# TensorE's order in two mixers: from the scheduler's to the emitted one, with new constants in the estimate behind it

## The chip, the cores and the metric

The kernel runs on one core of a Trainium2 chip. The metric is the device time of one execution in microseconds. Before the change the median of three runs is 2134.4 us (2134.18 to 2135.02). One further execution was profiled; every row shown comes from it.

The engines have short names in the rows: PE is TensorE's matrix products, PEld its weight loads, DVE is VectorE, ACT ScalarE, POOL GpSimd and SP the engine that issues the DMAs.

## The reference

The reference is a trunk of two layers for a sequence of 512 tokens of width 1024, in float32. A layer adds to its state half a gated feed-forward, then a mixer, then half a second gated feed-forward:

```
for layer in range(2):
    x = x + 0.5 * swiglu_ffn(x, pre weights)        # 1024 -> 2 x 2816 -> 1024
    u = rms_norm(x, mix_norm)
    x = x + mixer(u) @ w_out                        # A in layer 0, B in layer 1
    x = x + 0.5 * swiglu_ffn(x, post weights)
    if layer == 0: k_blocks, v_blocks = shared_kv_blocks(x)
```

Mixer A projects `u`, shifts the result by a token, and runs a linear recurrence over the 512 tokens for 12 heads of width 64:

```
sa    = einsum(state, -kk_t)
state = state * w_t + sa * (kk_t * a_t) + v_t * k_t
y_t   = einsum(state, r_t)
```

The output is normed per head and gated. Four more heads attend over 256 memory tokens. Mixer B has 12 heads of windowed attention with three dilations on the shared keys and values, and four memory heads.

## The kernel before

**Layout.** The state stands transposed, 128 features on the partitions and 512 tokens along them, in eight tiles. Every large product is split: a float32 operand becomes a high and a low part, and three products (high by high, high by low, low by high) are summed in PSUM. `dense` emits these triples. For each chunk of four 128 x 128 weight blocks it calls `weight`, which loads the raw chunk (SP, six buffers), copies it to `whi` on ScalarE and subtracts to `wlo`, on GpSimd in the mixers (four buffers each). After each triple it yields once.

**Mixer A.** The 12 heads are six pairs, called heads here. The recurrence is done in chunks of 64 tokens. `rwkv_prepare` makes the scaled operands of a head, `rwkv_solve` inverts a triangular matrix in five doubling levels, `rwkv_finish` steps through the eight chunks and norms the result. One level of the solve is: a transposition on VectorE (`tx<-TT`), sixteen 64 x 64 products on TensorE (`sc<-tx,mb`), a masked copy on VectorE (`tx<-sc,cst`), sixteen more products (`sc<-TT,tx`), and an addition on VectorE (`TT<-TT,sc`). Each float32 product stands in the trace as two rows, hence 32 rows to a block.

The mixer's work is written as eight generators, or strands: finish, two scans (solves of even and odd heads), prepare, two of memory attention, the projections, and a first pass of the output projection. `prepare` for head j waits until head j-2 is finished (`len(ys) > j - 2`), and the projections of head j wait until head j-2 is prepared.

**Mixer B.** Here the strands are memory attention, two of dilated attention, `settle` (norms and transpositions of the projections), the projections, and a first pass of the output projection.

**The order.** `weave` picks the strand to emit from. A strand that yields `WAIT` names the time at which its last results are expected; one that yields `FREE` can go on at once. The first strand in the list whose time has come is taken, and if there is none, the one that comes next. Time here is an estimate: `Meter` holds a clock for each of the four computing engines, and for each tile when it was last written and read. `note` advances them at each emitted instruction: it starts when its engine is free and its inputs are written, in the order of emission on every engine, and takes what `cost` says. The clock of TensorE is the present time of `weave`. DMAs and the loading of ScalarE's function tables are not in the estimate.

```
start = max([self.clock[engine], self.read.get(name, 0.0)] + [self.written.get(a.tensor.name, 0.0) for a in ins])
end = start + self.cost(engine, op, out, ins, sum(a.shape[-1] == 1 for a in ins))
```

**The compile-time scheduler.** The emitted program then goes through the scheduler of the language. It replays the program with a cost model of its own and gives each engine, whenever it is free there, the first emitted instruction that is ready. So an instruction can be moved ahead of earlier emitted ones. What comes out is a fixed order for each engine; on the chip an instruction waits for its semaphores, and those behind it on that engine wait with it. Before the change this holds for TensorE too. The feed-forward stages are emitted straight, without `weave`.

All instructions of the computing engines stand in the trace under line 278, that of the recording helper `Engine`; rows are told apart by their tiles: `mm` are the projections' PSUM tiles, `sc` those of the small steps, `py` those of the recurrence and of the attention outputs, `fps` those of the feed-forward; `uh`, `ul` and `kvh`, `kvl` are the split activations.

## Time and profile before

| | |
|---|---|
| median of three runs | 2134.4 us |
| the profiled execution: its time, its span | 2133.36 us, 2131.6 us |
| TensorE busy (products; weight loads) | 2065.4 us; 1651.9 us |
| VectorE, ScalarE, GpSimd busy | 983.3, 817.6, 583.1 us |
| mean granted clock of TensorE | 0.995 |
| instructions | 32197 |

The span runs from the first to the last instruction of the trace; the execution's own time has a little around it. Mixer A lies at about 385 to 800 us, mixer B at about 1545 to 1785 us, and the rest is feed-forward and the memory and key work beside it. A row that groups instructions gives their count, then busy time in us and the mean of one in ns, then the idle time just before them and what ended it. A row in order of time gives the start and the duration in us. Products overlap in TensorE's pipeline, so the distance of two starts says more than a duration.

### The profile page before, as it was taken

The page shows a single profiled execution, that of the slowest core. Times are in us where ns is not written, and L with a number is a line of the kernel's source. Part 1 is how long each engine was busy: PE and PEld are TensorE (multiplying, and loading weights), DVE is VectorE, ACT ScalarE, POOL GpSimd, SP SyncE. Part 2 cuts the span into 40 slices and gives each one's busy share as a digit, 9 for nine tenths or more (in the row PEclk, how much of TensorE's full clock was granted, in tenths as well). Part 3 has the DMA queues.
Part 4 walks back from the last instruction along what each step waited for, and adds up shares of the span by engine and source line. Part 5 has one row for each costly group of instructions (what it writes and reads, how often), then busy time and mean ns, then how long its engine had stood idle before and what let it go on. Part 6 is the DMA issues. An engine that isn't in the chain of part 4 may idle for free.

```text
span 2131.6 us, 32197 instructions
## 1 busy us (share of the span) xinstructions
PE 2065.4 (97%) x12734; PEld 1651.9 (77%) x12734; DVE 983.3 (46%) x1354; ACT 817.6 (38%) x1408; POOL 583.1 (27%) x502
## 2 busy tenths in 40 slices
PE   8999999979989899999999999999999999999999
PEld 6888888857666577778888888888877667888887
DVE  6333343575767747333434533324376675333322
ACT  6333333423333545333433433333345654333321
POOL 2222222643332133222222222222242224222221
PEclk9999999999999999999999999999999999999999
DMA  5322344311100045253344423234441144222342
GB/s 194 97 97 96 92 136 126 117 46 34 34 27 24 24 152 188 93 183 99 109 127 126 158 95 98 95 94 135 125 136 50 38 161 156 96 97 96 94 136 82
DMA packets 130632, 221.90 MB, mean 104 GB/s; under 512 B 14232, under 2 KB 31824, under 8 KB 130480
## 3 DMA queue, kind: packets, MB, share of 16 engines
q1 hardware_dynamic: 130480, 219.83, 32.8%
q8 instruction: 100, 1.64, 0.3%
q14 instruction: 52, 0.43, 0.1%
HBM read 202.89 MB, written 21.61 MB: 105 GB/s over the span
## 4 chain that ended last, share of the span: by engine, by line
PE 62%; DVE 2%; ACT 1%; issue 1%; DMA 0%; POOL 0%; SPq 0%; POOLq 0%; ACTq 0%; DVEq 0%
PE fps L278 50%; PE mm L278 6%; PE sc L278 4%; PE py L278 1%; DMA xin<-xd 0%; DVE prob L278 0%; DVE x L278 0%; DVE tmp L278 0%; DVE ul L278 0%; ACT krv L278 0%; DVE wlo L278 0%; DVE dmx L278 0%; POOL wlo L278 0%; DVE mpr L278 0%; ACT tmp L278 0%
## 5 line engine op out<-in xcount | busy, mean ns | idle before, releaser
L278 POOL TENSOR_TENSOR wlo<-raw,whi 128x512 fp32r<-128x512 f32 (+3 forms) x404 | 496.3, 1230 | 1439.7 <-ACT whi L278 1395.2
L278 ACT ACTIVATE whi<-raw 128x512 fp32r<-128x512 f32 (+3 forms) x684 | 416.1, 610 | 955.1 <-PE fps L278 778.7
L278 PE MATMUL fps<-uh,whi 128*128 128x512 f32 x1408 | 551.9, 392 | 7.6 <-ACT whi L278 7.6
L278 PE MATMUL fps<-uh,wlo 128*128 128x512 f32 x1408 | 550.0, 391 | 4.0 <-DVE wlo L278 2.4
L278 PE MATMUL fps<-ul,whi 128*128 128x512 f32 x1408 | 549.2, 390 | 0.0
L278 DVE TENSOR_TENSOR wlo<-raw,whi 128x512 fp32r<-128x512 f32 x280 | 201.2, 719 | 347.0 <-ACT whi L278 337.3
L278 PEld LDWEIGHTS fps<-uh,whi 128*128 128x128 f32 x1408 | 264.9, 188 | 68.3 <-ACT whi L278 11.1
L278 PEld LDWEIGHTS fps<-uh,wlo 128*128 128x128 f32 x1408 | 264.9, 188 | 62.0 <-DVE wlo L278 4.1
L278 PEld LDWEIGHTS fps<-ul,whi 128*128 128x128 f32 x1408 | 265.0, 188 | 56.0 <-issue 0.7
L278 PE MATMUL fps<-hh,whi 128*128 128x512 f32 x704 | 273.9, 389 | 0.0
L278 PE MATMUL fps<-hl,whi 128*128 128x512 f32 x704 | 273.9, 389 | 0.0
L278 PE MATMUL fps<-hh,wlo 128*128 128x512 f32 x704 | 273.9, 389 | 0.0
L278 DVE TENSOR_TENSOR gs<-fps,rstd 128x512 f32<-128x512 f32 x88 | 60.5, 690 | 322.9 <-PE fps L278 322.9
L278 PEld LDWEIGHTS fps<-hh,whi 128*128 128x128 f32 x704 | 132.1, 188 | 27.5
L278 PEld LDWEIGHTS fps<-hh,wlo 128*128 128x128 f32 x704 | 132.1, 188 | 27.4
L278 PEld LDWEIGHTS fps<-hl,whi 128*128 128x128 f32 x704 | 132.1, 188 | 27.4
L278 PE MATMUL mm<-uh,whi 128*128 128x512 f32 x280 | 120.6, 431 | 1.3 <-DVE x L278 0.9
L278 DVE TENSOR_TENSOR hm<-fps,gs 128x512 f32<-128x512 f32 x88 | 60.6, 691 | 121.5 <-PE fps L278 115.8
L278 PE MATMUL mm<-ul,whi 128*128 128x512 f32 x280 | 114.7, 410 | 1.1 <-DVE ul L278 1.1
L278 PE MATMUL mm<-uh,wlo 128*128 128x512 f32 x280 | 113.3, 405 | 0.0
L278 DVE RECIPROCAL tmp<-tmp 128x128 f32<-128x128 f32 x112 | 97.8, 918 | 29.1 <-ACT tmp L278 29.0
L278 DVE TENSOR_TENSOR hl<-hm,hh 128x512 fp32r<-128x512 f32 x88 | 76.9, 877 | 50.7 <-ACT hh L278 50.7
(256 smaller groups left out, 2115.5 us busy)
## 6 DMA issues: line engine op xcount, KB each, us to landing
raw<-w SPq DMA_DIRECT2D x512, 256.0 KB, 2.7
raw<-wa_in SPq DMA_DIRECT2D x44, 256.0 KB, 3.0
xd<-x SPq DMA_DIRECT2D x40, 256.0 KB, 3.8
tmp<-xd SPq DMA_DIRECT2D x32, 256.0 KB, 3.7
xin<-xd SPq DMA_DIRECT2D x32, 256.0 KB, 4.2
raw<-w_kv SPq DMA_DIRECT2D x24, 256.0 KB, 2.8
raw<-w SPq DMA_DIRECT2D x32, 128.0 KB, 2.3
raw<-wmem SPq DMA_DIRECT2D x16, 256.0 KB, 2.6
```

Of the source, the lines that this page charges most:

```text
L278: r = f(*args, **kw)
```

## The change

Two things change together.

- In `mixer_a` and `mixer_b` a manual schedule is opened for TensorE: inside it the scheduler keeps TensorE's instructions in the order in which they are emitted. The other engines are ordered by the scheduler as before, and so is TensorE outside the two mixers.
- The constants of `Meter.cost` are new, and so is the time from the end of an instruction to the use of its result: 0.22 us for all engines, where it was 0.2 for VectorE and 0.15 for the others. With the constants, the emitted order of both mixers changes, since `weave` goes by them.

```
             if op == "transpose":
-                return n * 0.00083 + 0.003
+                return n * 0.00083 + 0.013
             passes = 4 if ins[1].dtype == F32 else 1
             small = self.ways > 1
-            turn, self.small = 0.1 * (small != self.small), small
-            return turn + max(n * passes * 0.000417, 0.105) / self.ways + 0.003
+            turn, self.small = 0.09 * (small != self.small), small
+            return turn + (max(n * passes * 0.000417, 0.096) + 0.013) / self.ways
         if engine == "scalar":
-            return (0.05 if psum else 0.09) + 0.08 * extra + n * 0.00083
+            return (0.16 if psum else 0.21) + 0.08 * extra + n * 0.0008
         if engine == "gpsimd":
-            return 0.1 + n * (0.0022 if op.startswith("tensor_tensor") else 0.001)
+            return 0.19 + n * (0.00215 if op.startswith("tensor_tensor") else 0.001)
         if op == "reciprocal":
-            return 0.07 + n * 0.0063
-        fast = op in ("tensor_scalar", "tensor_copy") and not psum
-        return 0.07 + 0.06 * extra + n * (0.00052 if fast else 0.00104)
+            return 0.07 + n * 0.0064
+        if op in ("tensor_scalar", "tensor_copy") and not psum:
+            return 0.27 + n * 0.0003
+        return 0.142 + 0.06 * extra + n * (0.0021 if op == "tensor_tensor_scan" else 0.00107)
...
-        late = end + (0.15 if engine != "vector" else 0.2)
+        late = end + 0.22
...
     def mixer_a(...):
             pool = ctx.enter_context(tc.tile_pool(name="mixa", bufs=1, reuse_waits="tile"))
+            ctx.enter_context(tc.manual_schedule(engines={mybir.EngineType.PE}))
...
     def mixer_b(...):
             pool = ctx.enter_context(tc.tile_pool(name="mixb", bufs=1, reuse_waits="tile"))
+            ctx.enter_context(tc.manual_schedule(engines={mybir.EngineType.PE}))
```

## The prediction, on record before the result

> **What bounds the kernel now.** I read the totals first, then the forty slices, the busy time by stretches, the groups of instructions, and last the order of time inside one solve of mixer A.

> ```profile
> span 2131.6 us, 32197 instructions
> PE 2065.4 (97%) x12734; PEld 1651.9 (77%) x12734; DVE 983.3 (46%) x1354; ACT 817.6 (38%) x1408; POOL 583.1 (27%) x502
> PE   8999999979989899999999999999999999999999
> ```

> TensorE sets the time; the low digits stand in slices 9 to 15, which is mixer A. By stretches (us; then busy time and count of PE, weight loads, VectorE, ScalarE, GpSimd; granted clock; DMA):

> ```profile
> 420.00:720.00 300.00, 266.45 (x4035) 195.10 (x4033) 201.48 (x282) 100.95 (x179) 107.17 (x98) 0.97 0.10 31
> 720.00:750.00 30.00, 25.43 (x351) 17.74 (x352) 23.00 (x52) 19.93 (x51) 0.00 (x0) 1.00 0.12 37
> 1545.00:1755.00 210.00, 199.31 (x1075) 147.80 (x1075) 144.54 (x212) 110.40 (x210) 58.75 (x50) 1.00 0.30 93
> 675.00:700.00 25.00, 20.30 (x267) 13.86 (x265) 23.35 (x33) 9.60 (x14) 4.51 (x4) 1.00 0.07 22
> ```

> TensorE is idle for 300 - 266.45 = 33.6 us in the body of mixer A, 4.6 us in the next 30, and 210 - 199.31 = 10.7 us in mixer B. The feed-forward stages, which the change leaves alone, are full. Mixer A is no TensorE-bound stage: it is held by a loop. Head j+2 is prepared only after head j is finished (the wait in `prepare`), so prepare, solve and finish follow one another, two heads at a time. The solve has five levels for each of six heads, 30 in all, and each level is a closed chain:

> ```profile
> L278 PE MATMUL sc<-TT,tx 64*64 64x64 f32 x960 | 35.6, 225 | 7.5 <-DVE tx L278 7.4
> L278 PE MATMUL sc<-tx,mb 64*64 64x64 f32 x960 | 34.9, 221 | 10.0 <-DVE tx L278 7.4 <-ACT krv L278 1.9 <-ACT tmp L278 0.6
> L278 DVE STREAM_TRANSPOSE tx<-TT 128x512 f32<-128x512 f32 x30 | 21.0, 701 | 9.3 <-POOL TT L278 8.9
> L278 DVE TENSOR_TENSOR TT<-TT,sc 128x512 f32<-128x512 f32 x30 | 20.4, 680 | 19.1 <-PE sc L278 19.0
> L278 DVE TENSOR_TENSOR tx<-sc,cst 128x512 f32<-128x512 f32 x30 | 20.3, 675 | 12.4 <-PE sc L278 10.1 <-PE py L278 2.3
> ```

> A level cannot be shorter than 34.9/30 + 35.6/30 + 0.701 + 0.680 + 0.675 = 4.41 us and its hand-overs. What it takes beyond that is waiting: for VectorE, or in TensorE's queue behind dense products. The queue is what this change reorders. In order of time (start, duration; uh, ul, whi, wlo are dense products, tx,mb the first block of a level):

> ```profile
> 462.67 0.39 PE L278 MATMUL mm<-uh,whi 128*128 128x512 f32 x1
> 462.99 1.15 PE L278 MATMUL sc<-TT,tx 64*64 64x64 f32 x32
> 464.07 0.50 PE L278 MATMUL mm<-ul,whi 128*128 128x512 f32 x1
> 506.33 0.71 DVE L278 STREAM_TRANSPOSE tx<-TT 128x512 f32<-128x512 f32 x1
> 506.92 0.39 PE L278 MATMUL mm<-ul,whi 128*128 128x512 f32 x1
> 508.54 0.40 PE L278 MATMUL mm<-uh,wlo 128*128 128x512 f32 x1
> 508.77 1.02 PE L278 MATMUL sc<-tmp,cst 128*128 128x512 f32 x2
> 509.72 0.39 PE L278 MATMUL sc<-tx,mb 64*64 64x64 f32 x6
> ```

> The first three rows show that the order is not the emitted one. `dense` emits its three products without a yield between, so no block of a solve can stand between the first and the second of them by emission; the compile-time scheduler put it there. The other rows show the price of its guess: the transposition is over at 507.04, and the block that needs it starts at 509.72, 2.68 us later, with dense products queued ahead and then a statistics product of another strand.

> **The change, part by part.**

> *The order on TensorE.* No instruction is added or taken away in either mixer: the same products, splits and DMAs. Only their places in TensorE's queue differ, and, through the emission order, the priorities by which the scheduler still orders the other engines. SP's loads keep their queue; a raw weight lands in 3.0 us here and six buffers run ahead, so I cost the DMAs at nothing (row below); without that cover a chunk would show the 3.0 us.

> ```profile
> raw<-wa_in SPq DMA_DIRECT2D x44, 256.0 KB, 3.0
> 451.52 0.71 DVE L278 STREAM_TRANSPOSE tx<-TT 128x512 f32<-128x512 f32 x1 [2.18 <-POOL TT L278]
> 452.38 0.41 PE L278 MATMUL sc<-tx,mb 64*64 64x64 f32 x7 [2.13 <-DVE tx L278]
> 751.70 0.70 DVE L278 STREAM_TRANSPOSE tx<-TT 128x512 f32<-128x512 f32 x1
> 752.73 0.45 PE L278 MATMUL sc<-tx,mb 64*64 64x64 f32 x8
> ```

> The gain is priced on these pairs. From the end of a level's transposition to its block, the first of the 30 pairs has 0.15 us, the last 0.33, the one above 2.68; the mean over all 30, taken from the same rows, is 1.02 us. After the change nothing can stand before such a block that the estimate did not put there, and dense work comes in whole triples. From 506.92 to 508.54 eight consecutive dense products start, so they are 1.62/7 = 0.23 us apart and a triple is 0.69; a block that finds a triple running waits half of it, 0.34 us. That is 30 x (1.02 - 0.34) = 20.4 us off the loop. Bounds: 0, if the estimate puts as much ahead as the scheduler did, and 30 x (1.02 - 0.15) = 26 us, if every pair becomes like the first. I take 20, because the long waits come in whole groups of dense products that emission would not place. The second block of a level, the prepares and the finishes I leave at no change.

> *The new constants.* They are near the trace: 0.142 + 512 x 0.00107 = 0.69 us for a product on VectorE against 0.68 shown; 0.21 + 512 x 0.0008 = 0.62 on ScalarE against 0.63 below; 0.19 + 512 x 0.00215 = 1.29 on GpSimd against 1.38 in mixer A. What they cannot know:

> ```profile
> L278 DVE SCALAR_TENSOR_TENSOR tmp<-krv,vec,tmp 128x512 f32<-128x512 f32 x6 | 9.0, 1502 | 0.1
> L278 DVE SCALAR_TENSOR_TENSOR beta<-tmp,tmp 128x512 f32<-128x512 f32 x6 | 8.3, 1376 | 0.1
> L278 ACT ACT_TABLE_LOAD x16 | 20.5, 1283 | 2.7 <-PE sc L278 2.4
> L278 ACT ACTIVATE whi<-raw 128x512 fp32r<-128x512 f32 x45 | 28.1, 629 | 81.4 <-PE mm L278 70.0 <-issue 6.7 <-POOL p L278 3.4
> L278 POOL TENSOR_TENSOR wlo<-raw,whi 128x512 fp32r<-128x512 f32 x46 | 63.3, 1379 | 120.3 <-ACT whi L278 91.4 <-PE mm L278 16.1 <-ACT WU L278 9.9
> ```

> Two steps of each prepare take 1.50 and 1.38 us where the estimate says 0.69, so it calls them ready 6 x (0.81 + 0.69) = 9 us too early over the six heads, and it leaves out 16 table loads of 1.283 us. Where TensorE's next instruction waits for such a step, all dense products behind it wait too, now with no scheduler to pull them ahead. In mixer A such waits lie on the loop already, whichever order TensorE has, and TensorE's 33.6 idle us cover the dense work that is pushed back; I cost them at nothing. If that cover is gone, they cost up to 9 + 20.5 = 29.5 us there.

> [...]

> *The weight splits in the estimate.* This is the weak point. The estimate keeps ScalarE, VectorE and GpSimd in emission order. A weight chunk split behind a ScalarE step that has just ended is taken to be ready only after its copy, its subtraction and two hand-overs of 0.22 us. The real scheduler starts splits early. In mixer B:

> ```profile
> L278 ACT ACTIVATE whi<-raw 128x512 fp32r<-128x512 f32 (+1 forms) x54 | 30.5, 566 | 45.3 <-PE mm L278 34.0 <-issue 6.8 <-POOL wlo L278 4.1
> L278 POOL TENSOR_TENSOR wlo<-raw,whi 128x512 fp32r<-128x512 f32 (+1 forms) x53 | 61.5, 1162 | 153.1 <-ACT whi L278 151.9 <-DMA tmp<-xd 1.1
> L278 PE MATMUL mm<-kvh,whi 128*128 128x512 f32 x116 | 48.7, 420 | 2.3 <-DVE x L278 2.3
> L278 PE MATMUL mm<-kvh,wlo 128*128 128x512 f32 x116 | 45.6, 393 | 0.0
> ```

> The believed wait is up to 0.566 + 1.162 + 0.44 = 2.17 us a chunk, while the products on wlo wait 0.0 us in fact. So TensorE reaches the chain step emitted behind sooner than the estimate thinks, and waits there. If half of the 53 splits meet this, at half the wait, it is 26.5 x 1.08 = 29 us. The lower bound is a gain of 10.7 us, all the idle time of mixer B. I take +6, nearer to the lower end: 26.5 x 0.22, one hand-over for each such split, since the estimate also makes the chain steps too long (0.22 against the 0.15 us of the first pair above), which works the other way. In mixer B this counts in full, since TensorE is 95% busy there.

> **Sum.** -20.4 + 6 = -14.4 us. Against the profiled execution's 2133.36 us (span 2131.6 and 1.8 around it) that is 2119.0; the median, 2134.4, is 1.0 above that execution, so the forecast is **2120 us**.

> **Rivals.**

> *Slower: the estimate's own waits become TensorE's.* Place: mixer B, where each waiting step now has the dense products behind it. Price: the full 29 us, while of mixer A's 20.4 us only a third is left, 6.8, since there too a step that is called ready too early blocks the other strand's step: 2134.4 + 29 - 6.8 = 2157. It decides once mixer B loses more than mixer A gains, from 20.4/29 = 0.7 of that price on with A's gain whole, from 0.23 with a third of it. For it: the 0.0 us row, with nothing left that can fill. Against it: the constants for the chain steps match the rows.

> *No change.* VectorE, not TensorE's queue, holds the levels: it is busy 23.35 of 25 us at 675 to 700, and a block that starts earlier then meets a later transposition. With a gain of 6 us in A and a loss of 6 in B: 2134. Against it: over 420 to 720 VectorE is busy 201.48 of 300 us only. That the order stays as it was is out, by the split triple above.

> *A larger gain.* The prepares and finishes gain as the solves do, and half of the idle time in all three stretches goes, 0.5 x (33.6 + 4.6 + 10.7) = 24 us; the lost clock, 0.03 x 300 = 9 us of the first stretch, goes with it: 2134.4 - 33 = 2101. For it: long waits of one queue entry behind another strand's. Against it: most of that idle time lies on the loop itself. [...]

> **Chances and range.** Forecast 0.38, larger gain 0.16, no change 0.13, slower 0.33. A measurement of this kernel tells 0.2%, some 4 us, from no change. Faster is 0.38 + 0.16 = 0.54, same 0.13, slower 0.33. The two ends of the unknown costs, with A at -26 and B at -10.7, and with A at 0 and B at +29, give 2098 and 2163; I take 2098 to 2162. The likeliest case's own range is 2108 to 2129.

> **What would show it.** Right: no block of a solve inside a triple; the mean from transposition to first block near 0.35 us; mixer A some 20 us shorter; mixer B's end within 10 us of its old length. Wrong in the first term: that mean still near 1 us, or mixer A no shorter. Wrong in the second: mixer B's idle time well above 10.7 us, with waits of products behind steps of ScalarE or VectorE while dense work is left. The forecast falls if mixer B loses more than mixer A wins.

## The result, and the profile after

The changed kernel takes **2193.84 us** (median of four runs, 2191.45 to 2195.44), against 2134.6 us for the kernel before beside it. The ratio is **1.0263**, 95% interval 1.0245 to 1.028: 59 us slower. The forecast was 2120 us, 14 us faster, and the range ended at 2162. The first lines of the page after:

```profile
span 2193.7 us, 32202 instructions
PE 2085.3 (95%) x12734; PEld 1672.0 (76%) x12734; DVE 979.4 (45%) x1354; ACT 816.6 (37%) x1406; POOL 578.6 (26%) x502
PE   8999999989897899999999999999998888999999
PEclk9999999999899899999999999999999899999999
```

The count of product rows is the same, 12734. The span has grown by 2193.7 - 2131.6 = 62.1 us. TensorE's idle time went from 2131.6 - 2065.4 = 66.2 to 2193.7 - 2085.3 = 108.4 us, so **42.2 us are new idle time** and the other **19.9 us are busy time**: the same products took longer. The low digits of the PE row are in mixer A, as before, and now also in mixer B (slices 31 to 34). The other three engines have no more work than before.

Timed from its first projection product to the first feed-forward product after it, mixer A went from 419.4 to 451.4 us (+32.0) and mixer B from 218.2 to 247.4 us (+29.1, from the rows below). Together that is 61.1 of the 62.1 us. Busy time over each whole mixer shows both kinds of loss in both places (us; busy time and count of PE, weight loads, VectorE, ScalarE, GpSimd; granted clock; DMA). Before:

```profile
385.95:805.39 419.44, 380.03 (x5062) 279.77 (x5061) 270.81 (x396) 160.30 (x303) 151.24 (x148) 0.98 0.18 58
1545.72:1763.95 218.23, 207.54 (x1111) 154.56 (x1110) 153.02 (x222) 118.44 (x226) 65.05 (x57) 1.00 0.31 100
```

After; the third row is the later part of mixer B alone:

```profile
386.57:837.99 451.42, 392.46 (x5062) 292.34 (x5061) 268.02 (x396) 160.87 (x303) 146.53 (x148) 0.93 0.17 55
1577.88:1825.25 247.37, 213.08 (x1112) 160.27 (x1111) 157.68 (x226) 118.45 (x227) 70.43 (x60) 0.93 0.28 90
1640.00:1815.00 175.00, 148.49 (x847) 111.58 (x844) 110.72 (x174) 88.79 (x180) 35.96 (x34) 0.91 0.21 69
```

In mixer A idle time went from 39.4 to 59.0 us and busy time grew by 12.4 us. In mixer B idle time went from 10.7 to 34.3 us and busy time grew by 5.5 us. The granted clock fell from 0.98 to 0.93 in mixer A and from 1.00 to 0.93 in mixer B.

What TensorE waited for in mixer A (product and its releaser: us in total, times, longest), before and after:

```profile
PE sc L278 <- DVE tx L278: 14.8, 14, 2.1
PE sc L278 <- DVE tmp L278: 5.9, 2, 5.5
PE py L278 <- DVE G L278: 1.6, 1, 1.6
PE py L278 <- ACT H L278: 1.3, 6, 0.2
```

```profile
PE sc L279 <- DVE tx L279: 25.9, 19, 3.0
PE sc L279 <- DVE tmp L279: 8.6, 3, 5.5
PE py L279 <- DVE G L279: 5.2, 2, 2.9
PE py L279 <- ACT H L279: 4.3, 10, 0.4
```

Two steps of VectorE write a tile named `tx`: the transposition and the masked copy. The rows of the two blocks, shown in the prediction and in experiment 4, part them: the waits for the transposition went from 7.4 to 17.9 us, and those for the masked copy, the rest, from 7.4 to 8.0 us.

And in mixer B, before and after:

```profile
PE sc L278 <- DVE mpr L278: 4.2, 4, 1.7
PE sc L278 <- DVE prob L278: 2.2, 4, 1.2
```

```profile
PE sc L279 <- DVE mpr L279: 14.4, 5, 5.3
PE sc L279 <- DVE prob L279: 8.0, 5, 5.7
PE sc L279 <- ACT whi L279: 3.3, 1, 3.3
PE sc L279 <- POOL wlo L279: 2.7, 1, 2.7
```

No new kind of wait has come: the steps that TensorE waits for most are those it waited for before, only longer; at the end of mixer B two late weight splits come to them. One of the longest shows how. In order of time, the logits of a memory head (`sc<-memkv,tmp`) and the transposition of its probabilities (`sc<-cst,mpr`), before:

```profile
1638.82 1.13 PE L278 MATMUL sc<-memkv,tmp 64*128 64x256 f32 x8
1639.89 0.50 PE L278 MATMUL mm<-uh,whi 128*128 128x512 f32 x1
...
1642.21 0.40 PE L278 MATMUL mm<-ul,whi 128*128 128x512 f32 x1
1642.88 0.66 PE L278 MATMUL sc<-cst,prob 128*128 128x128 f32 x4 [0.26 <-ACT mpr L278]
1643.29 0.48 PE L278 MATMUL mm<-uh,wlo 128*128 128x512 f32 x1
...
1645.79 1.14 PE L278 MATMUL sc<-cst,mpr 128*128 128x128 f32 x8
```

and after:

```profile
1669.06 1.72 PE L279 MATMUL sc<-memkv,tmp 64*128 64x256 f32 x8 [1.30 <-DVE prob L279]
1670.71 0.50 PE L279 MATMUL mm<-uh,whi 128*128 128x512 f32 x1
1671.05 0.40 PE L279 MATMUL mm<-ul,whi 128*128 128x512 f32 x1
1671.28 0.39 PE L279 MATMUL mm<-uh,wlo 128*128 128x512 f32 x1
1676.95 1.94 PE L279 MATMUL sc<-cst,mpr 128*128 128x128 f32 x8 [5.27 <-DVE mpr L279]
```

The softmax between takes about as long in both: 7.0 us from start to start before, 7.9 after. Before, the scheduler had put more than four triples and other strands' products there, splitting a triple at 1642.88, so that TensorE waited 0.26 us. After, the emission had put one triple there, and TensorE waits 5.27 us with the other triples queued behind the transposition.

### The profile page after: what moved, and what is told of

The parts are those of the page before. It is cut to its first block, busy times and chain, and to the rows that moved or that the text cites. A ratio compares the mean times of both kernels' runs of the same rounds, so it can differ in the third digit from the quotient of the medians.

```text
span 2193.7 us, 32202 instructions
## 1 busy us (share of the span) xinstructions
PE 2085.3 (95%) x12734; PEld 1672.0 (76%) x12734; DVE 979.4 (45%) x1354; ACT 816.6 (37%) x1406; POOL 578.6 (26%) x502
## 4 chain that ended last, share of the span: by engine, by line
PE 61%; DVE 3%; ACT 1%; issue 1%; POOL 0%; DMA 0%; POOLq 0%; DVEq 0%; ACTq 0%
PE fps L279 50%; PE mm L279 6%; PE sc L279 4%; PE py L279 1%; DVE tmp L279 1%; DVE prob L279 1%; POOL sq L279 0%; DVE mpr L279 0%; DVE dmx L279 0%; DVE mx L279 0%; POOL wlo L279 0%; ACT mpr L279 0%; DVE x L279 0%; DVE tx L279 0%; ACT prob L279 0%
## 5 line engine op out<-in xcount | busy, mean ns | idle before, releaser
L279 PE MATMUL mm<-uh,whi 128*128 128x512 f32 x280 | 127.5, 455 | 1.0 <-DVE x L279 0.6
## 6 DMA issues: line engine op xcount, KB each, us to landing
raw<-w SPq DMA_DIRECT2D x512, 256.0 KB, 2.7
raw<-wa_in SPq DMA_DIRECT2D x44, 256.0 KB, 2.9
xd<-x SPq DMA_DIRECT2D x40, 256.0 KB, 3.1
tmp<-xd SPq DMA_DIRECT2D x32, 256.0 KB, 3.8
xin<-xd SPq DMA_DIRECT2D x32, 256.0 KB, 4.3
raw<-w_kv SPq DMA_DIRECT2D x24, 256.0 KB, 2.8
raw<-wmem SPq DMA_DIRECT2D x16, 256.0 KB, 2.7
```

Of the source, the lines that this page charges most:

```text
L279: r = f(*args, **kw)
```

## The experiments

Two things had to be told apart first: the constants and the fixed order. Then, what in the fixed order costs the time. **Theory W**: the estimate believes in waits for weight splits that TensorE does not have, so it emits too little dense work ahead of each step. **Theory F**: a fixed place for the dense products costs time however the estimate is made, since it is their freedom that fills TensorE's waits. The expectations name three more. **C**: the estimate makes the chain steps too short. **K**: the constants themselves make a bad order. **S**: the emitted order of the small steps is itself worse. Mixer durations below are measured as above, one profiled execution each.

**1. The two parts, each alone.** The constants without the fixed order:

```
             pool = ctx.enter_context(tc.tile_pool(name="mixa", ...))
-            ctx.enter_context(tc.manual_schedule(engines={mybir.EngineType.PE}))
...
             pool = ctx.enter_context(tc.tile_pool(name="mixb", ...))
-            ctx.enter_context(tc.manual_schedule(engines={mybir.EngineType.PE}))
```

> New constants alone; the scheduler may reorder TensorE again. Theory W (the fixed order carries the estimate's false waits for weight splits onto the chip) and theory C (it carries too short chain steps) both say that the scheduler mends the order: mixer A near 419 us, mixer B near 218, 2126 to 2145 us. Theory K (the constants themselves make a bad order) says over 2170.

Measured: ratio to the kernel before 0.9997 (0.9987 to 1.0007), mixer A 418.1 us, mixer B 224.3 us. Theory K is out. Mixer B, expected near 218 us, is 6 us longer in the one execution that was profiled, which the ratio does not show. And the fixed order with all the old constants, two of which are shown:

```
 class Meter:
...
-            return (0.16 if psum else 0.21) + 0.08 * extra + n * 0.0008
+            return (0.05 if psum else 0.09) + 0.08 * extra + n * 0.00083
...
-        late = end + 0.22
+        late = end + (0.15 if engine != "vector" else 0.2)
```

> Fixed TensorE order with the old constants. W: the old constants hold the same false waits, a little shorter, so nearly the same loss, 2165 to 2200 us. C: the old constants make the chain steps shorter still, by about 0.1 us an instruction, so the loss is larger than with the new ones, 2200 to 2230. K: near 2135.

Measured: 1.0266 (1.0248 to 1.0285), mixer A 450.6 us, mixer B 245.4 us. The median, 2195.14 us, lies in the range of W and below that of C. The fixed order is the whole loss. The new constants, nearer to the trace or not, change nothing that can be measured in the whole time, with either order.

**2. The fixed order in mixer A alone.**

```
     def mixer_b(...):
             pool = ctx.enter_context(tc.tile_pool(name="mixb", ...))
-            ctx.enter_context(tc.manual_schedule(engines={mybir.EngineType.PE}))
```

> New constants, TensorE's order fixed in mixer A alone. All theories: the parts add, mixer A stays at 451 us, mixer B returns to about 218, 2165 us within 5. Much less than 2160 would say that mixer B's start depends on A's end; much more that the new constants alone hurt B.

Measured: 1.0147 (1.0122 to 1.0172), 32 us over the kernel before, mixer A 457.2 us, mixer B 222.3 us, as with the constants alone. Each mixer loses by itself; about half of the 59 us belongs to either. Mixer A is the same here as in the changed kernel and took 5.8 us more, so a single execution does not tell its duration to better than that.

**3. The weight splits out of the estimate.** Only the estimate changes: the splits are emitted as before but not noted, so weights count as ready.

```
+        real = self.tc.nc
-        nc.scalar.activation(hi, raw, AF.Copy)
+        real.scalar.activation(hi, raw, AF.Copy)
...
-        eng = nc.vector if self.split % 2 and not self.busy_vector else nc.gpsimd
+        eng = real.vector if self.split % 2 and not self.busy_vector else real.gpsimd
```

> As the changed kernel, but the estimate leaves the weight splits out (the instructions stay, on the same engines): a dense product is never believed to wait for its weights. W: more dense work stands ahead of each chain step, mixer A 410 to 430 us, mixer B 213 to 225, 2125 to 2150 us in all. C: the chain steps are still too short in the estimate, so most of the loss stays, 2175 us or more.

Measured: 1.0240 (1.0224 to 1.0255), an interval that overlaps that of the changed kernel. But the two mixers moved apart: mixer B fell from 247.4 to 230.7 us, mixer A rose from 451.4 to 464.4 us. By Theory W both should have gained. It holds for part of mixer B, 16.7 of its 29.1 us, and fails in mixer A: with more dense work emitted ahead, the mean over the 30 levels from the end of the transposition to its block is 1.39 us (0.99 in the changed kernel), and mixer A loses more clock, not less (0.89 against 0.93). The total lies where Theory C put it; experiment 5 tests that theory. The two mixers in this run:

```profile
385.63:850.02 464.39, 399.59 (x5061) 300.76 (x5060) 265.36 (x396) 160.32 (x303) 146.29 (x148) 0.89 0.17 53
1589.46:1820.12 230.66, 206.79 (x1112) 157.62 (x1110) 153.36 (x222) 116.41 (x225) 65.33 (x57) 0.96 0.30 95
```

**4. The steps in the order of emission, the dense products free.** The manual schedule is taken out, and each product of a strand other than the projections and the first pass of the output projection is tied to the one emitted before it by an ordering dependence that holds at compile time alone. The scheduler may then put dense products anywhere between.

```
+def weave(meter, strands, tc, free):
...
+    def tie(r):
+        ins = getattr(r, "ins", r)
+        if last:
+            tc.add_manual_dep(ins, last[0].name, mybir.DependencyInfo(mybir.DependencyClass.NoSync, mybir.DependencyReason.DATA), reason="order")
+        last[:] = [ins]
...
-            ctx.enter_context(tc.manual_schedule(engines={mybir.EngineType.PE}))
...
-            weave(self.meter, [memory(), dilated(0), dilated(1), settle(), projections(), first_pass()])
+            weave(self.meter, [memory(), dilated(0), dilated(1), settle(), projections(), first_pass()], tc, (4, 5))
```

> New constants; only the small steps (all strands but the projections and the first pass) are tied to their emitted order among themselves, the dense products are free to go between them. Theory F (the loss is that dense work can no longer be pulled ahead of a waiting step): the loss goes, 2130 to 2150 us, mixer A 415 to 428, mixer B 217 to 226. Theory S (the emitted order of the small steps of several strands is itself worse, one strand's waiting step blocks another's ready one): the loss stays, 2170 us or more.

Measured: 1.0015 (1.0000 to 1.0030), mixer A 420.5 us, mixer B 223.5 us, all three in the ranges of Theory F. In the trace of mixer B the `sc` blocks of the small steps start in the same sequence as in the changed kernel; with the constants alone they do not. This settles it against Theory S: the steps' fixed order costs 3 us of the 59 (6 by the interval's upper end); the fixed places of the dense products, with what the scheduler then makes of the other engines' order, cost the rest. That any fixed place must cost this much is not shown: the manual schedule with the dense products emitted where the scheduler had put them was not run. The groups of instructions show the same in one row, the first block of a level, whose idle time is the first figure behind the second bar. It was 10.0 us before; with the constants alone it is

```profile
L279 PE MATMUL sc<-tx,mb 64*64 64x64 f32 x960 | 35.7, 226 | 12.4 <-DVE tx L279 10.0 <-ACT krv L279 1.9 <-ACT tmp L279 0.6
```

with the steps in order and the dense products free

```profile
L280 PE MATMUL sc<-tx,mb 64*64 64x64 f32 x960 | 36.3, 228 | 12.5 <-DVE tx L280 10.1 <-ACT krv L280 1.9 <-ACT tmp L280 0.6
```

and in the changed kernel

```profile
L279 PE MATMUL sc<-tx,mb 64*64 64x64 f32 x960 | 35.2, 224 | 20.7 <-DVE tx L279 17.9 <-ACT krv L279 1.9 <-ACT tmp L279 0.6
```

**5. A longer hand-over in the estimate**, which makes each chain look longer and so puts more dense work before its next step.

```
-        late = end + 0.22
+        late = end + 0.6
```

> As the changed kernel, with 0.6 us instead of 0.22 from the end of an instruction to the use of its result in the estimate. If the chain steps are estimated too short, more dense work ahead of each helps: mixer A below 440, mixer B below 235, 2150 to 2175 us. If the false waits for weights rule, they grow as well (two hand-overs to a split) and nothing is won: 2185 to 2205 us.

Measured: 1.0285 (1.0259 to 1.031), mixer A 463.4 us, mixer B 235.5 us. Mixer B gains 11.9 us, mixer A loses as much, so Theory C is not borne out in mixer A. The mean from transposition to block is 0.96 us there, no longer than in the changed kernel, and TensorE waits longer for the transpositions, 26.7 us:

```profile
L279 PE MATMUL sc<-tx,mb 64*64 64x64 f32 x960 | 37.6, 233 | 29.4 <-DVE tx L279 26.7 <-ACT krv L279 2.4 <-ACT tmp L279 0.2
```

> Both: no weight splits in the estimate and 0.6 us for each hand-over. If false waits and short steps together are the fault of mixer B, it comes to 218 to 225 us here. In mixer A a gain (below 440) would say that its steps are called ready too early; a further loss (over 464) that dense work placed ahead of its chain is what costs there.

Measured with both edits: 1.0366 (1.0339 to 1.0393), mixer A 484.5 us, mixer B 236.3 us, not the 218 to 225 that were expected; the mean from transposition to block in mixer A is 2.14 us. So an estimate that asks for more dense work ahead does not mend mixer A. In the two versions without the splits the steps wait longer for TensorE (1.39 and 2.14 us); with 0.6 us alone they do not, and why mixer A grows there was not found. None of the lengths that were tried repairs it; shorter ones, 0.15 and 0.2 us, were tried only together with the old constants (experiment 1).

**6. The waits of mixer B filled with products that compute nothing.** In the changed kernel, 15 products of the constant tile go into the bank that the waiting block then overwrites, before four blocks that wait, the longest of them 5.7 us. All of the kernel's own work is done.

```
+    def keep(self, ps, n):
+        for _ in range(n if self.in_b else 0):
+            self.tc.nc.tensor.matmul(ps, self.same, self.cst[:, :T], start=True, stop=True)
...
                 pt = bank("sc", (P, 2, MEM))
+                if not e:
+                    self.keep(pt.rearrange("p k u -> p (k u)"), {(0, 0): 4, (1, 0): 2, (1, 1): 4}.get((j, h), 0))
...
                         turn = bank("sc", (P, 4, P))
+                        if unit == 4 and not i:
+                            self.keep(turn.rearrange("p x u -> p (x u)"), 5)
```

> The changed kernel, order and constants as they are; only before four of the waiting blocks of mixer B (three on mpr, one on prob) TensorE gets 15 extra products of the constant tile into the same bank, which the block then overwrites, some 0.95 us each at full clock, so that it works while it waits 5.3, 3.0, 5.4 and 6.0 us. It leaves nothing out. Theory clock: about half of what mixer B lost is the half clock that follows the waits. Changed kernel: granted clock 0.91 over the 175 us from 1640, so 0.09 x 175 = 15.8 us. With the waits filled the clock goes to about 0.98 to 1.00, mixer B from 247 to 232 to 238 us, the whole ratio from 1.026 to 1.019 to 1.022. Rival, idle alone: the clock costs nothing that the waits do not hide again, so whatever the clock shows, mixer B stays at 245 to 250 us and the ratio at 1.025 to 1.028.

Measured: 1.024 (1.0223 to 1.0257), mixer B 239.2 us instead of 247.4, at a granted clock of 0.97 instead of 0.93; the second row is its middle stretch, at 0.98:

```profile
1580.38:1819.62 239.24, 220.66 (x1141) 160.21 (x1140) 157.67 (x226) 117.67 (x227) 70.36 (x60) 0.97 0.29 93
1643.00:1808.00 165.00, 153.19 (x867) 109.49 (x864) 109.45 (x173) 86.53 (x178) 34.54 (x33) 0.98 0.22 70
```

Products that do no work made mixer B 8.1 us shorter, though they can shorten no wait. That speaks for the clock and against the rival, by which mixer B would have stayed at 245 us or more. It rests on one profiled execution of each; the changed kernel and the one with the old constants, whose mixer B is fixed too, are 2 us apart there. It is less than expected (9 to 15 us). The ratio missed its range of 1.019 to 1.022 too: mixer A, where nothing was changed, took 2.7 us more in this execution, and the ratio's interval overlaps that of the changed kernel. The verdict therefore rests on mixer B's own duration and clock.

No version that was run is faster than the kernel before.

## Why the prediction was wrong, step by step

**The first term, 30 x (1.02 - 0.34) = 20.4 us off the loop, did not happen.** The mean from the end of a level's transposition to its block is 0.99 us after, against 1.02 before. Nor does this wait tell the slow versions from the others: it is 0.97 us with the constants alone and 0.94 us with the steps in order and the dense products free. What was foreseen of the form is there: no block of a solve stands inside a triple, and dense work comes in whole triples. The step that failed is "the long waits come in whole groups of dense products that emission would not place". Emission places them. In order of time, the transposition that ends at 508.65 + 0.71 = 509.36 and its block:

```profile
508.65 0.71 DVE L279 STREAM_TRANSPOSE tx<-TT 128x512 f32<-128x512 f32 x1
509.36 1.02 PE L279 MATMUL sc<-tmp,cst 128*128 128x512 f32 x2
509.82 0.79 PE L279 MATMUL mm<-uh,whi 128*128 128x512 f32 x1
...
512.30 1.02 PE L279 MATMUL sc<-tmp,cst 128*128 128x512 f32 x2
513.25 1.15 PE L279 MATMUL sc<-tx,mb 64*64 64x64 f32 x32
```

Between them stand three triples and two statistics products, 3.89 us, a longer wait than the 2.68 us that the prediction showed as the price of the scheduler's guess. The lower bound of the term, 0, named the reason: the estimate puts as much ahead as the scheduler did. That was the right end.

**The idle time of mixer A, costed at nothing, is the second failed step.** The prediction said that TensorE's 33.6 idle us cover the dense work that is pushed back. They do not: idle time grew by 19.6 us and mixer A by 32.0. An average of idle time in a stretch is no cover, since dense work fills a wait only if it stands in the queue at that place, and in the fixed order the wait stands ahead of it, as in the 5.27 us shown above. The price written for "if that cover is gone", 29.5 us, was near 32.0 in size, but for another reason. It was made of two slow steps and the table loads, while the waits that grew most are those on the transpositions, 7.4 to 17.9 us; that the price came near the loss is luck. The loop that the prediction described passes the delay on. The first and the last of the six heads' finishes, before and after:

```profile
522.10 0.65 DVE L278 TENSOR_TENSOR y<-sc,tmp 128x512 f32<-128x512 f32 x1
...
783.87 0.69 DVE L278 TENSOR_TENSOR y<-sc,tmp 128x512 f32<-128x512 f32 x1
```

```profile
529.02 0.68 DVE L279 TENSOR_TENSOR y<-sc,tmp 128x512 f32<-128x512 f32 x1
...
810.70 0.69 DVE L279 TENSOR_TENSOR y<-sc,tmp 128x512 f32<-128x512 f32 x1 [1.62 <-PE sc L279]
```

The first head ends 6.9 us later and the last 26.8 us.

**The third term, +6 us for the weight splits in mixer B, was mis-sized.** Mixer B measured +29.1, the full upper bound of 29. The mechanism is real but is not all of it: without the splits in the estimate mixer B is still 12.4 us longer than before (230.66 against 218.23). That the upper bound was met is partly luck, since the price held waits alone and 5.5 of the 29.1 us are busy time. The place that the slower rival named, each waiting step with the dense products behind it, is what the rows of mixer B show. It should have carried the sum.

**The lost clock was weighed on one side only.** It stood in the larger gain, as 9 us to be won back. It went the other way: the granted clock of mixer A fell from 0.98 to 0.93, that of mixer B from 1.00 to 0.93, and 19.9 us of the 62.1 are busy time of the same products. That the 9 us, 0.03 of the first stretch, would come back whole was the author's estimate, and no run shows it; what a run shows is that mixer B's clock rose from 0.93 to 0.97 when four of its waits were filled (experiment 6). How long TensorE had been idle when the clock fell differs from wait to wait: in mixer B 3.1 us into a wait of 5.27 us, 3.4 us into one of 4.96 us and 1.6 us into the longest, 5.74 us; in mixer A 1.9 us into one of 2.27 us (last section).

**The rivals.** The slower one had the sign, the place in mixer B and its price, 29 us. Its other half failed: of mixer A's gain not a third was left but nothing, and mixer A lost as much again. With +29 and +32 in place of +29 and -6.8 its sum, 2134.4 + 61, is near the 2193.84 that was measured. Its own sum, 2157, was still 37 us short. "No change" was set aside on the split triple alone: that the order changed was right. Of the marks named in advance, those for "wrong" came in: mixer A no shorter, the mean near 1 us, mixer B's idle time at 34.3 against 10.7 us, with waits behind steps of ScalarE and VectorE while dense work is left. That the DMAs cost nothing is nearly so: no wait of TensorE is directly on one, but the first of the two late weight splits at the end of mixer B goes back to a late load. TensorE waits 3.28 us for it, from 1816.65 to 1819.93; its load was issued at 1814.83 and landed 3.7 us later, at 1818.5, and ScalarE copied the chunk at 1819.48, behind two other steps.

**What stays open.** How the 32 us of mixer A divide between idle time that lengthens the loop and half clock that lengthens the steps in it was not separated by a run; the rows of the whole mixer show 19.6 us more idle time and 12.4 us more busy time. Mixer B took 222 to 224 us in all three versions that have the new constants and leave its dense products free, against 218.2 us before, one execution each; so up to 6 of its 29.1 us may not be the fixed order's.

## What to carry to other kernels

Where long work that can run at any time shares an in-order queue with short steps of a latency chain, leave the long work free to move; here fixing the order of the short steps alone cost next to nothing (1.0015), and fixing both cost 2.6%. Do not count an engine's idle time as cover for work that stands behind a wait in its queue. And price a lost clock on both sides: here new waits came with a granted clock of 0.93 in both mixers, where it had been 0.98 and 1.00, and with 19.9 us more busy time for the same products.

## What the runs showed of the hardware that was not expected

```profile
541.59:545.00 3.41, 1.48 (x92) 1.34 (x83) 3.41 (x6) 0.71 (x2) 1.94 (x3) 1.00 0.12 35
545.00:548.41 3.41, 1.80 (x28) 1.23 (x28) 3.41 (x5) 0.94 (x3) 0.00 (x0) 0.50 0.14 51
548.41:551.83 3.42, 1.83 (x32) 1.11 (x24) 0.83 (x2) 1.33 (x5) 1.28 (x2) 0.50 0.00 0
551.83:555.24 3.41, 2.07 (x2) 0.50 (x2) 0.98 (x2) 0.52 (x2) 0.00 (x0) 0.50 0.00 0
```

In order of time, the recurrence's steps with no dense product between them:

```profile
545.34 0.48 PE L279 MATMUL py<-H,G 64*64 64x64 f32 x4 [2.27 <-DVE G L279]
546.22 0.37 PE L279 MATMUL py<-pt,H 64*64 64x64 f32 x2 [0.40 <-ACT H L279]
...
552.15 2.07 PE L279 MATMUL sc<-tmp,cst 128*128 128x512 f32 x2 [0.60 <-ACT tmp L279]
```

Most of one wait of 2.27 us lies in the first stretch. With waits of about 0.4 us following, TensorE is busy for 1.80, 1.83 and 2.07 us of the next three stretches, the clock stays at half, and the statistics product takes 2.07 us, twice the 1.02 us that it took at 509.36. In the two mixers of this trace the clock falls 16 times, each time after a stretch of 3.41 us in which TensorE was busy for at most 0.54 of the time, and only one of these stretches was wholly idle. Products that compute nothing, put into four waits of mixer B, shortened it by 8.1 us, at a granted clock of 0.97 instead of 0.93.
